# Hybrid decoder layer: second-layer input parts split from SBUF in two lumps, filler and early rows spread anew

## The chip, the core and the metric

The kernel runs on one core of a Trainium2 chip. The metric is the device time of one execution in microseconds (us); lower is better. One execution is also recorded by the hardware profiler, and its times are counted from the start of its span. The engines are named as in the profile: PE (TensorE, matmul), PEld (its weight loads), DVE (VectorE), ACT (ScalarE), POOL (GpSimd), SP (SyncE, which issues all the transfers of this kernel).

## The reference

One decoder layer over 1024 tokens of width 1024, all in float32:

```
h  = rmsnorm(x, g_pre);  proj = h @ W_in       # q,k,v of attention; q,f,i,g of the recurrence
A  = rmsnorm(dilated_attention(q_a, k_a, v_a)) # 8 heads of 64
     # three patterns (window, dilation): (128,1), (512,4), (2048,16), causal, ALiBi bias,
     # combined by their softmax denominators
R  = hgrn2(q_h, f_h, i_h, lb)                  # 4 heads of 128
     # S_t = diag(f_t) S_{t-1} + (1-f_t) i_t^T ; o_t = S_t^T q_t ; rmsnorm per head, times silu(g)
x  = x + rmsnorm(concat[A, R] @ W_out, g_post)
x  = x + rmsnorm(relu(rmsnorm(x, g_mlp) @ W1)^2 @ W2)     # W1: 1024 x 4096
```

## The kernel before

**Numbers and tiles.** A tile has 128 partitions. Each large product is made of three matmuls on two float32r parts of each operand, a rounded copy `hi` and the remainder `lo` (`three_pass`, L86 to L89: hi·hi, hi·lo, lo·hi). The parts are made by `split_into` (L82 to L84): a copy on ACT, then a subtraction on DVE. Weights come by SP into `raw`, are split into `wh` and `wl`, and the next one is loaded when a split has been issued (`w_split`, `w_get`); a weight either takes a rotating pair of `wh`/`wl`, or slabs named for it (`WO_TAG` for the eight blocks of W_out). Slabs are tiles of one size that several uses share one after the other: S 9, T 9, P 3, BT 2, V8 2, R 1, and eight larger ones ("A"). PSUM has four tags of two banks each: mm, s, t, pv.

**Order of the work.** The program is written out in order and each engine runs its part of it in that order. Work that isn't urgent, mostly projections, is a Python generator in `queue`. `fill(ns)` takes steps from it until their nominal costs (650 for three 128x512 matmuls) reach the amount; `drain()` takes all that is left. So `fill` and `drain` settle where the matmuls of the projections stand between those of the main work. A generator may also give up the turn when it has to wait for a place.

**Stages.** (1) Norm of the input and projections of head 0. (2) The four recurrence heads: `hgrn_core` (L373) makes the diagonal product `pd` from `prod` by eight small matmuls, then the levels within chunks (`pl`), transposes (`pk`), the states (`pu`, `st`), the outputs (`po`) in two groups and the gated norm; the filler is the next head's projections, and for the last head those of the first attention pair. Results go to `mix_dram` in DRAM. (3) Attention, 64 iterations, `s` = head times 8 + query block `b`, two heads to a pair. An iteration issues the exponential of block s+1 (`raise_`, ACT L577), the scores of s+2 (`look`, matmuls `ps` L563, maximum `mx` on DVE L566), the transposes of block s's probabilities (`turn`, `pt` L590, split into `pth` L593 on ACT and `ptl` L594 on DVE), every other iteration the weighted sum of values (`weigh`, `pov` L607, copied as `ot` L610), later the sum over two halves (`finish`, `fold` L618, L621), then a hook of that iteration and `fill`. The filler is `attn_proj`: V, K and Q of the next pair; K's half `kf` (L521) is split by ACT (`kh` L523) and POOL (`kl`), and copied to the other 64 partitions by four transfers. At the last iteration but one of a pair, `drain` runs ahead of the first scores of the next pair, which read `pairs`. (4) Output projection. The recurrence part of token blocks 0 to 3 is made early: `early_open` (L638) loads `erows` (L643), POOL multiplies them by the gain `gmix` (`row_rec` L658), PE transposes them (`row_turn`, `pmt` L698), and `early_out` makes the products `pwe` as filler in the last pair. Behind attention a loop over the eight token blocks makes the rest (`late_out`, `pwo`), the norm and residual (`residual`, `residual_b`, `esum` L775) and `next_turn`: transposes `ph` (L785) of the next layer's input, copied as `hraw` (L791), and for blocks 0 to 3 split into `h2` parts. (5), (6) The two feed-forward products, from L800 on; not touched.

The hooks at iterations 45 to 63 load the weights of W_out (`w_get(WO0 + k)`) and do the steps of (4) one by one.

Of the kernel before, what the change touches and what calls it, by code (L numbers as in the profile page):

```python
# [8 lines left out]
F32 = mybir.dt.float32  # L9
# [8 lines left out]
P = 128  # L18
# [7 lines left out]
AH = 8  # L26
# [4 lines left out]
def f32(ap):  # L31
    return ap.bitcast(F32)
# [3 lines left out]
def hymba_layer(ctx, tc, x, w_in, w_out, w_ff1, w_ff2, g_pre, lb_logits, g_mix, g_post,  # L36
# [40 lines left out]
    def rsqrt_mean(dst, ssum, n, width):  # L77
        t = col("ms", width)
        G.tensor_scalar(t, ssum, 1.0 / n, EPS, op0=ALU.mult, op1=ALU.add)  # L79
        G.tensor_tensor(out=dst, in0=t, in1=nhalf[:, :width], op=ALU.pow)  # L80
# [70 lines left out]
    for i in range(4 * HH, 4 * HH + 3 * (AH // 2)):  # L151
        stream.append((w_in[i], None))
    WO0 = len(stream)
    WO_TAG = (None, None, ("S", "S"), ("S", "BT"), ("S", "S"), ("S", "T"), ("T", "T"), ("T", "T"))

    def wo_dest(k, tags):
        return lambda: (slab(tags[0], f"woh{k}", F32R), slab(tags[1], f"wol{k}", F32R))
# [215 lines left out]
    def hgrn_core(h, scale, after=None):  # L373
        hd = heads[h]
        inat, gate, prod, qt, kt, tot = (hd[n] for n in ("inat", "gate", "prod", "qt", "kt", "tot"))
        fill(4500 * scale)
        pd = bank("t", f"pd{h}")
        for c in range(NT):
            TE.matmul(pd[:, c:c + 1], prod[:, c * P:(c + 1) * P], ones, start=True, stop=True)
# [3 lines left out]
        V.tensor_tensor(out=at, in0=ident.unsqueeze(1).to_broadcast([P, NT, P]),  # L383
                        in1=dg.unsqueeze(2).to_broadcast([P, NT, P]), op=ALU.mult)
        cur = tot
        for li, c in enumerate(LEVELS):
            nb = 64 // c
            qv = qt.rearrange("p (b two c) -> p b two c", two=2, c=c)
            kv = kt.rearrange("p (b two c) -> p b two c", two=2, c=c)
            av = at.rearrange("p n (b two c) -> p n b two c", two=2, c=c)  # L390
            pl = bank("s", f"pl{h}_{li}")
            for n in range(NT):
                TE.matmul(pl[:, n * 64:(n + 1) * 64], kt[:, n * P:(n + 1) * P],  # L393
                          qv[:, n * nb:(n + 1) * nb, 1, :], start=True, stop=True)
            w = T // (2 * c)
            cv = cur[:, :2 * w].rearrange("p (b two) -> p b two", two=2)
            V.tensor_tensor(out=kv[:, :, 0, :], in0=kv[:, :, 0, :],
                            in1=cv[:, :, 1:2].to_broadcast([P, w, c]), op=ALU.mult)
            V.tensor_tensor(out=qv[:, :, 1, :], in0=qv[:, :, 1, :],  # L399
                            in1=cv[:, :, 0:1].to_broadcast([P, w, c]), op=ALU.mult)  # L400
            nx = slab("P", f"tot{h}_{w}") if w > 64 else \
                tp.tile([P, w], F32, tag=f"tot{w}", name=f"tot{h}_{w}", bufs=1)
            V.tensor_tensor(out=nx[:, :w], in0=cv[:, :, 0], in1=cv[:, :, 1], op=ALU.mult)
            V.copy_predicated(
                av[:, :, :, 1, :],
                masks[:, li].rearrange("p (b c) -> p b c", c=c).unsqueeze(1).to_broadcast([P, NT, nb, c]),
                pl.rearrange("p (n b c) -> p n b c", n=NT, c=c))
            cur = nx
            fill(2900 * scale)
# [26 lines left out]
        for g4 in range(2):  # L436
            po = bank("pv", f"po{h}_{g4}").rearrange("p (n c) -> p n c", n=4)
            for j in range(4):
                n = g4 * 4 + j
                TE.matmul(po[:, j], at[:, n], inat[:, n], start=True, stop=n == 0)  # L440
                if n > 0:
                    TE.matmul(po[:, j], qt[:, n * P:(n + 1) * P], st[:, n], start=False, stop=True)
            g = slice(g4 * 4, g4 * 4 + 4)
            S.activation(sq[:, g], po, AF.Square)
            V.tensor_reduce(ss[:, g], sq[:, g], axis=AX.X, op=ALU.add)  # L445
            pos.append(po)
        rsqrt_mean(rs, ss, P, NT)
        if after is not None:
            after()
        fill(3000 * scale)  # L450
        for n in range(NT):
            V.scalar_tensor_tensor(gate[:, n], pos[n // 4][:, n % 4], rs[:, n:n + 1], gate[:, n],
                                   op0=ALU.mult, op1=ALU.mult)
# [8 lines left out]
    def attn_proj(pr):  # L462
# [48 lines left out]
        for hf in range(2):  # L511
            sl = slice(hf * 512, hf * 512 + 512)
            n = 0
            for cost in proj_t(w, f"ak{pr}", hf, box):
                n += 1
                if n == 3 and hf == 0:
                    v_turn(*late)
                    cost += 450.0
                yield cost
            full = half(f"kf{pr}{hf}")  # L520
            V.tensor_tensor(out=full, in0=box[0], in1=rrow[:, sl], op=ALU.mult)  # L521
            for i, (a, b) in enumerate(halves):
# [3 lines left out]
            for n in ("kh", "kl"):  # L526
                nc.sync.dma_start(out=f32(stacks[0][n][64:128, sl]), in_=f32(stacks[0][n][0:64, sl]))
                nc.sync.dma_start(out=f32(stacks[1][n][0:64, sl]), in_=f32(stacks[1][n][64:128, sl]))
            yield 650.0
        pairs[pr] = (stacks, vs)  # L530

    anats = [None] * (AH // 2)
    bts = {}
# [2 lines left out]

    def load_bias(hd):
        if hd < AH and hd not in bts:
            if hd < AH - 1:
                bts[hd] = slab("BT", f"bt{hd}")  # L540
            else:
                bts[hd] = wide.tile([P, 2, T], F32, tag="A", name=f"bt{hd}")[:, 0]
            nc.sync.dma_start(out=bts[hd], in_=bias_tab[hd])

    def score(hd, b):
# [89 lines left out]
    NE = 4  # L635
    early = {}

    def early_open():  # L638
        early["rows"] = wide.tile([P, NE, AW], F32, tag="A", name="erows")
        early["mt"] = [wide.tile([P, 2, 2, 4, P], F32R, tag="A", name=f"emt{q}") for q in range(NE // 2)]  # L640
        load_bias(AH - 1)
        early["sum"] = [wide.tile([P, 2, D], F32, tag="A", name=f"esum{q}") for q in range(NE // 2)]
        nc.sync.dma_start(out=early["rows"],  # L643
                          in_=mix_dram[:NE * P, :AW].rearrange("(n p) d -> p n d", p=P))

    def early_sum(t):
        return early["sum"][t // 2][:, t % 2]
# [7 lines left out]
        return early["rows"][:, t] if t < NE else rows[t][:, :AW]  # L655

    def row_rec(t):
        G.tensor_tensor(out=rec_row(t), in0=rec_row(t), in1=gains["gmix"][:, :AW], op=ALU.mult)  # L658

    def row_fin(t):  # L660
        return anats[-1][:, t].rearrange("p i d -> p (i d)")
# [115 lines left out]
    def next_turn(t):  # L777
# [3 lines left out]
        for kh in range(2):  # L781
# [7 lines left out]
                if th == 0:  # L789
                    h2[kh] = tuple(wide.tile([P, 4, 512], F32R, tag="A", name=f"h2{q}{kh}") for q in "hl")  # L790
            S.activation(hraw[kh, th][:, :, c:c + P], src, AF.Copy)  # L791
            if th == 0:
                hi, lo = (q[:, :, c:c + P] for q in h2[kh])
                split_into(hi, lo, src)

    steps = [(hd, b) for hd in range(AH) for b in range(NT)]
    scored, exped = {}, {}
# [19 lines left out]
    for h in range(HH):  # L817
# [6 lines left out]
            drain()  # L824

    hooks = {
        45: lambda: [drain(), load_gain("gmix", "R", g_mix), early_open()],
        46: lambda: w_get(WO0, 0),
        47: lambda: [w_get(WO0 + 1, 0), row_rec(0), row_rec(1)],
        48: lambda: [row_turn(0, 0), w_get(WO0 + 2, 0), row_rec(2), row_rec(3)],  # L830
        49: lambda: [row_turn(1, 0), w_get(WO0 + 3, 0), queue.extend(early_out(t) for t in range(NE))],
        50: lambda: row_turn(2, 0),
        51: lambda: row_turn(3, 0),
        55: lambda: [row_load(t) for t in range(3)],
        59: lambda: [row_norm(0), row_gain(0)],
        60: lambda: [row_norm(1), row_gain(1)],
# [6 lines left out]
    for s in range(n_steps):  # L843
# [10 lines left out]
            to_weigh.append((hd, b // 2))  # L854
        to_fold, last_fold = [(i, g, weigh(i, g)) for i, g in ready], to_fold
        if fresh and s + 2 < n_steps:
            drain()
            if (s + 2) // 16 + 1 < AH // 2:
                queue.append(attn_proj((s + 2) // 16 + 1))
            look(s + 2)  # L860
        for i, g, a in last_fold:
            finish(i, g, *a)
        hooks.get(s, lambda: None)()
        fill(2700.0 - 320.0 * b if s < n_steps - 16 else 1300.0)
    for i, g, a in to_fold:
        finish(i, g, *a)
    to_fold = [(i, g, weigh(i, g)) for i, g in to_weigh]
# [11 lines left out]
    for t in range(NT):  # L879
# [16 lines left out]
        if t + 3 < NT:  # L896
            row_norm(t + 3)
            if t + 3 < NE:
                row_gain(t + 3)
        if t == 4:  # L900
            w_get(W10, 0)
        mixed_half(t, 1)
# [758 lines left out]
```

## Time and profile before

| | |
|---|---|
| three runs | 1313.2, 1319.82, 1316.15 us |
| median | 1316.15 us |
| the profiled execution | 1313.2 us, span 1311.4 us (1.8 us lie around it) |
| PE busy | 1264.5 us, 96% of the span, 6730 matmul instructions |
| DVE, ACT, POOL busy | 858.7, 515.1, 283.6 us |
| mean granted clock over the span | 0.99 |

By the spans of the stages in the profiled execution, the recurrence heads run from about 42 to 300 us, the last of them ends near 336 us, attention runs until about 590 us, and the output projection until about 675 us.

In a row of instructions the first number is the time it starts (us), the second its duration; then engine, line, operation, `out<-in` with the program's names, shape, and in square brackets the time its engine had been idle just before and what it waited for last. A row of a group has its count, the busy time, the mean duration of one in ns, and the idle time before. The granted clock is the share of full speed at which TensorE was clocked in that stretch.

### The profile page before, as it was taken

To read this page: it belongs to the slowest core of one execution; us is meant where nothing else is said; L and a number is where in the kernel's file an instruction comes from. 1 tells how busy PE (TensorE), PEld (TensorE's weight loads), DVE (VectorE), ACT (ScalarE), POOL (GpSimd) and SP (SyncE) were. 2 spreads that over 40 slices of the span, in tenths; PEclk is the share of its full clock that TensorE was granted. 3 is DMA by queue.
4 is the path that set the end of the run, shared out by engine and by line. 5 is a ranking of instruction groups with operands and counts; after the bars stand their busy time and mean duration, and the time that the engine had idled before them with its cause. 6 is when DMAs were issued, how large, how long until landed. Compare 5 with 4: busy or idle time off the path is not lost. (4 is left out here: it accounts for less than half of the span.)

```text
span 1311.4 us, 17500 instructions
## 1 busy us (share of the span) xinstructions
PE 1264.5 (96%) x6730; PEld 1081.8 (82%) x6730; DVE 858.7 (65%) x1431; ACT 515.1 (39%) x908; POOL 283.6 (22%) x276
## 2 busy tenths in 40 slices
PE   9999999999989999898999899999999999999997
PEld 8898989888878888786887688888887888888886
DVE  5556566675656655666757656666666777688956
ACT  6612121213545554564555422222234633344412
POOL 0000000012011111123432178755651000000002
PEclk9999999999999999899999899999999999999999
DMA  5202020213122222416251444534469453444423
GB/s 203 65 17 65 17 64 17 65 49 98 48 81 65 81 65 59 137 41 215 97 177 58 143 168 169 177 129 140 174 222 347 165 196 115 146 131 128 147 80 130
DMA packets 58563, 153.77 MB, mean 117 GB/s; under 512 B 5104, under 2 KB 13040, under 8 KB 58224
## 3 DMA queue, kind: packets, MB, share of 16 engines
q1 hardware_dynamic: 58480, 152.66, 34.9%
q8 instruction: 53, 0.87, 0.3%
q14 instruction: 30, 0.25, 0.1%
HBM read 106.50 MB, written 39.85 MB: 112 GB/s over the span
## 5 line engine op out<-in xcount | busy, mean ns | idle before, releaser
L88 PE MATMUL f<-bl,ah 128*128 128x512 f32 x392 | 152.6, 389 | 0.5 <-DVE bl L84 0.5
L87 PE MATMUL f<-bh,ah 128*128 128x512 f32 x392 | 152.6, 389 | 0.4 <-ACT acc L1441 0.4
L89 PE MATMUL f<-bh,al 128*128 128x512 f32 x392 | 152.5, 389 | 0.0
L84 DVE TENSOR_TENSOR al<-ar,ah 128x1024 fp32r<-128x1024 f32 x49 | 60.7, 1239 | 49.6 <-ACT ah L83 21.7
L88 PEld LDWEIGHTS f<-bl,ah 128*128 128x128 f32 x392 | 73.6, 188 | 16.1 <-DVE bl L84 0.8
L87 PEld LDWEIGHTS f<-bh,ah 128*128 128x128 f32 x392 | 73.6, 188 | 16.0 <-ACT acc L1441 0.9
L89 PEld LDWEIGHTS f<-bh,al 128*128 128x128 f32 x392 | 73.6, 188 | 15.3
L83 ACT ACTIVATE ah<-ar 128x1024 fp32r<-128x1024 f32 x49 | 52.3, 1067 | 54.1 <-PE f L89 25.3
L566 DVE CUSTOM_DVE_ANT_0 p<-ps,bt 128x512 f32<-128x512 f32 (+2 forms) x96 | 50.6, 552 | 31.7 <-PE ps L564 31.5
L1577 POOL TENSOR_SCALAR fp<-fss 128x1 f32<-128x1 f32 x8 | 3.5, 432 | 268.8 <-ACT fd L1574 268.8
L594 DVE TENSOR_TENSOR ptl<-pt,pth 128x512 fp32r<-128x512 f32 (+2 forms) x96 | 50.2, 551 | 16.4 <-ACT pth L593 16.3
L593 ACT ACTIVATE pth<-pt 128x512 fp32r<-128x512 f32 (+2 forms) x96 | 43.3, 486 | 42.0 <-PE pt L590 41.8
L590 PE MATMUL pt<-ident,p 128*128 128x128 f32 x288 | 43.6, 279 | 11.6 <-DVE ptl L594 11.6
L393 PEld LDWEIGHTS pl<-qt,kt 128*128 128x128 f32 x448 | 52.9, 192 | 1.5 <-PE pm_av L89 0.9
L393 PE MATMUL pl<-qt,kt 128*128 128x64 f32 x448 | 53.5, 272 | 0.5 <-DVE qt L399 0.5
L577 ACT ACTIVATE p<-p,nm 128x128 f32<-128x128 f32 (+3 forms) x64 | 49.5, 773 | 10.0 <-DVE nm L572 5.7
L524 POOL TENSOR_TENSOR kl<-kf,kh 64x512 fp32r<-64x512 f32 x16 | 20.4, 1274 | 151.3 <-ACT kh L523 150.7
L231 ACT ACTIVATE inat<-pig,rstd 128x128 f32<-128x128 f32 x32 | 11.6, 367 | 95.4 <-PE pig L89 82.3
L590 PEld LDWEIGHTS pt<-ident,p 128*128 128x128 f32 x288 | 33.7, 142 | 17.2 <-DVE ptl L594 14.2
L83 ACT ACTIVATE bh<-br 128x1024 fp32r<-128x1024 f32 x28 | 29.9, 1067 | 41.1 <-PE f L89 35.8
L79 POOL TENSOR_SCALAR ms<-hss 128x8 f32<-128x8 f32 x4 | 0.8, 196 | 203.6 <-DVE hss L445 203.6
L84 DVE TENSOR_TENSOR wl<-raw,wh 128x1024 fp32r<-128x1024 f32 x23 | 31.3, 1359 | 18.0 <-ACT wh L83 18.0
(1584 smaller groups left out, 3848.9 us busy)
## 6 DMA issues: line engine op xcount, KB each, us to landing
ar<-actd SPq DMA_DIRECT2D x49, 512.0 KB, 3.7
raw<-in_w_in_dram SPq DMA_DIRECT2D x28, 512.0 KB, 3.7
w1r<-in_w_ff_dram SPq DMA_DIRECT2D x14, 1024.0 KB, 6.5
br<-in_w_ff_dram SPq DMA_DIRECT2D x14, 1024.0 KB, 6.5
actd<-e SPq DMA_DIRECT2D x17, 768.0 KB, 4.2
actd<-e SPq DMA_DIRECT2D x11, 1024.0 KB, 4.1
xr<-in_x_dram SPq DMA_DIRECT2D x8, 512.0 KB, 9.0
bt<-in_bias_tab_dram SPq DMA_DIRECT2D x8, 512.0 KB, 4.3
```

What stands on the lines that cost most here:

```text
L83: S.activation(hi, src, AF.Copy)
L84: eng.tensor_tensor(out=lo, in0=src, in1=f32(hi), op=ALU.subtract)
L87: TE.matmul(dst, lhs[0], rhs[0], start=start, stop=False)
L88: TE.matmul(dst, lhs[0], rhs[1], start=False, stop=False)
L89: TE.matmul(dst, lhs[1], rhs[0], start=False, stop=stop)
L393: TE.matmul(pl[:, n * 64:(n + 1) * 64], kt[:, n * P:(n + 1) * P], qv[:, n * nb:(n + 1) * nb, 1, :], start=True, stop=True)
L524: G.tensor_tensor(out=stacks[i]["kl"][a:b, sl], in0=full[a:b], in1=f32(stacks[i]["kh"][a:b, sl]), op=ALU.subtract)
L566: V.tensor_tensor_reduce(out=pe[:, k0:k0 + n], in0=pS[:, :n], in1=bts[hd][:, o:o + n], scale=1.0, scalar=-3.0e38, op0=ALU.add, op1=ALU.max ...
L577: S.activation(pe[:, :nk], pe[:, :nk], AF.Exp, bias=nm[:, b:b + 1], accum_out=dn[:, b:b + 1])
L590: TE.transpose(pt[:, j * P:(j + 1) * P], pe[:, jj * P:(jj + 1) * P], ident)
L593: S.activation(hi, src, AF.Copy)
L594: V.tensor_tensor(out=lo, in0=src, in1=f32(hi), op=ALU.subtract)
```

## The change

Six edits.

1. In `hgrn_core`, the filler ahead of `pd` is cut in two, one part now behind `pd`; that ahead of the gated norm is cut in two as well, one part now between the two groups of `po`.
2. Two blocks of W_out exchange where their parts lie.
3. In attention, an iteration's filler is 3400 - 360b in place of 2700 - 320b up to iteration 43, 1000 in 44 to 47, and 1300 from there on as before.
4. `pairs[pr]` is set just before the last step of the generator, and the pair's end calls the filler until it is set; it is drained only when another pair's projection follows.
5. The rows of blocks 0 to 3 are loaded by `early_rows`, called from within the last pair's projection after the first half of K, in two transfers, with a copy of the gain's first half of their own in a tile that head 7's bias shares; the hooks that follow move one or two iterations.
6. `next_turn` keeps only `hraw`; `split_tokens` splits two blocks at a time from SBUF in iterations 4 and 6 of the output loop.

```diff
-    WO_TAG = (None, None, ("S", "S"), ("S", "BT"), ("S", "S"), ("S", "T"), ("T", "T"), ("T", "T"))
+    WO_TAG = (None, ("S", "S"), None, ("S", "BT"), ("S", "S"), ("S", "T"), ("T", "T"), ("T", "T"))
...
-        fill(4500 * scale)
+        fill(2200 * scale)
         pd = bank("t", f"pd{h}")
...
         cur = tot
+        fill(2300 * scale)
         for li, c in enumerate(LEVELS):
...
             pos.append(po)
+            if g4 == 0:
+                fill(1500 * scale)
...
-        fill(3000 * scale)
+        fill(1500 * scale)
...
+            if hf == 0 and pr == AH // 2 - 1:
+                early_rows()
             full = half(f"kf{pr}{hf}")
...
+            pairs[pr] = (stacks, vs)
             yield 650.0
-        pairs[pr] = (stacks, vs)
...
-    def early_open():
+    def early_rows():
         early["rows"] = wide.tile([P, NE, AW], F32, tag="A", name="erows")
+        early["table"] = wide.tile([P, 2, T], F32, tag="A", name="etable")
         early["mt"] = [wide.tile([P, 2, 2, 4, P], F32R, tag="A", name=f"emt{q}") for q in range(NE // 2)]
-        load_bias(AH - 1)
+        gains["early"] = early["table"][:, 1, :AW]
+        nc.sync.dma_start(out=gains["early"], in_=g_mix[:AW].partition_broadcast(P))
+        for q in range(NE // 2):
+            nc.sync.dma_start(out=early["rows"][:, 2 * q:2 * q + 2],
+                              in_=mix_dram[2 * q * P:2 * (q + 1) * P, :AW].rearrange("(n p) d -> p n d", p=P))
+
+    def early_sums():
         early["sum"] = [wide.tile([P, 2, D], F32, tag="A", name=f"esum{q}") for q in range(NE // 2)]
-        nc.sync.dma_start(out=early["rows"],
-                          in_=mix_dram[:NE * P, :AW].rearrange("(n p) d -> p n d", p=P))
...
             S.activation(hraw[kh, th][:, :, c:c + P], src, AF.Copy)
-            if th == 0:
-                hi, lo = (q[:, :, c:c + P] for q in h2[kh])
-                split_into(hi, lo, src)
+
+    def split_tokens(kh, c):
+        hi, lo = (q[:, :, c:c + 2 * P] for q in h2[kh])
+        split_into(hi, lo, hraw[kh, 0][:, :, c:c + 2 * P])
...
-        45: lambda: [drain(), load_gain("gmix", "R", g_mix), early_open()],
-        46: lambda: w_get(WO0, 0),
-        47: lambda: [w_get(WO0 + 1, 0), row_rec(0), row_rec(1)],
-        48: lambda: [row_turn(0, 0), w_get(WO0 + 2, 0), row_rec(2), row_rec(3)],
-        49: lambda: [row_turn(1, 0), w_get(WO0 + 3, 0), queue.extend(early_out(t) for t in range(NE))],
-        50: lambda: row_turn(2, 0),
-        51: lambda: row_turn(3, 0),
+        45: lambda: [row_rec(0), row_rec(1)],
+        46: lambda: [w_get(WO0, 0), row_rec(2), row_rec(3)],
+        47: lambda: [row_turn(0, 0), w_get(WO0 + 1, 0), load_bias(AH - 1)],
+        48: lambda: [drain(), load_gain("gmix", "R", g_mix), early_sums(), w_get(WO0 + 2, 0), row_turn(1, 0),
+                     queue.extend(early_out(t) for t in range(NE))],
+        49: lambda: [w_get(WO0 + 3, 0), row_turn(2, 0)],
+        50: lambda: row_turn(3, 0),
...
         if fresh and s + 2 < n_steps:
-            drain()
+            while pairs[(s + 2) // 16] is None:
+                fill(1.0)
             if (s + 2) // 16 + 1 < AH // 2:
+                drain()
                 queue.append(attn_proj((s + 2) // 16 + 1))
             look(s + 2)
...
-        fill(2700.0 - 320.0 * b if s < n_steps - 16 else 1300.0)
+        fill(3400.0 - 360.0 * b if s < n_steps - 20 else 1000.0 if s < n_steps - 16 else 1300.0)
...
+        if t in (4, 6):
+            for kh in range(2):
+                split_tokens(kh, (t - 4) * P)
```

More of the change, by code (lines that the diff above doesn't have):

```diff
@@ L657, in row_rec @@
     def row_rec(t):
-        G.tensor_tensor(out=rec_row(t), in0=rec_row(t), in1=gains["gmix"][:, :AW], op=ALU.mult)
+        gain = gains["early"] if t < NE else gains["gmix"][:, :AW]
+        G.tensor_tensor(out=rec_row(t), in0=rec_row(t), in1=gain, op=ALU.mult)
     def row_fin(t):
```

5 lines of the change are left out of this document (1 added, 4 removed).

## The prediction

> **What bounds the kernel now.** I read the page's head first, then the stretches by engine and granted clock, then the chain of waits of TensorE. Columns of a stretch: its length; PE, PEld, DVE, ACT and POOL busy us with instructions; granted clock; DMA share; GB/s. A row of waits has the total, the count and the longest.
>
> ```profile
> span 1311.4 us, 17500 instructions
> ...
> PE 1264.5 (96%) x6730; PEld 1081.8 (82%) x6730; DVE 858.7 (65%) x1431; ACT 515.1 (39%) x908; POOL 283.6 (22%) x276
> ...
> L84 DVE TENSOR_TENSOR al<-ar,ah 128x1024 fp32r<-128x1024 f32 x49 | 60.7, 1239 | 49.6 <-ACT ah L83 21.7
> ...
> L83 ACT ACTIVATE ah<-ar 128x1024 fp32r<-128x1024 f32 x49 | 52.3, 1067 | 54.1 <-PE f L89 25.3
> ```
>
> ```profile
> 340.00:540.00 200.00, 183.56 (x1080) 160.22 (x1080) 116.22 (x371) 100.47 (x223) 30.55 (x24) 0.96 0.26 74
> 600.00:675.00 75.00, 70.01 (x345) 57.06 (x343) 50.75 (x69) 38.51 (x104) 27.14 (x58) 1.00 0.37 126
> ```
>
> ```profile
> PE pt L590 <- DVE ptl L594: 11.6, 7, 2.8
> ```
>
> TensorE is busy 96% of the span, and the change removes no matmul. Time can come only from TensorE's gaps and from its clock. The attention stretch holds 16.4 idle us at a mean clock of 0.96, and the gaps there have names: seven waits of the probability transposes `pt` for `ptl`, the low half of the block before, and the wait of `pmt` for POOL (part 5). All of them sit where a pair of heads ends and the generator queue has run dry or is drained at once. I go through the places in order of time; a plus is time gained.
>
> **1. Recurrence.** The 4500 of filler before the diagonal product `pd` become 2200 before and 2300 behind it.
>
> ```profile
> 130.26 0.28 PE L87 MATMUL pig<-wig2h,hTh 128*128 128x256 f32 x1
> ...
> 132.78 0.28 PE L87 MATMUL pig<-wig2h,hTh 128*128 128x256 f32 x1
> 132.95 0.69 DVE L369 TENSOR_TENSOR prod<-qt,kt 128x512 f32<-128x512 f32 x1
> ```
>
> The `pig` matmuls of the filler run from 130.26 to 132.78, 21 in all. The second half of `prod`, which `pd` needs, ends at 132.95 + 0.69 = 133.64. With half of the filler gone, `pd` is reached some 0.36 early: an estimate, the rest of the first half and four `pd` before it being taken off the 3.4 us between. Three heads have filler: 3 x 0.36 = -1.1. The low bound is -3 x 0.69, a whole `prod` each; the high bound is 0, since TensorE had work here and nothing it waited for. The second split, 3000 into 1500 and 1500 around the group of `po`, keeps the same matmuls under the same norms: 0. If that cover were gone, it would cost the 0.69 of one such vector operation.
>
> **2. Opening of attention.** The first iterations get 3400 in place of 2700, which is two groups of three 128x512 matmuls more, by 650 each.
>
> ```profile
> 128.45 0.39 PE L88 MATMUL pm_f<-hTl,wh 128*128 128x512 f32 x1
> 128.68 0.39 PE L89 MATMUL pm_f<-hTh,wl 128*128 128x512 f32 x1
> ...
> 336.27 0.50 PE L563 MATMUL ps<-kh,q 128*128 128x512 f32 x1 [2.28 <-DVE mx L566]
> ```
>
> A 128x512 matmul starts every 0.23 us. Six more of them fill 6 x 0.23 = 1.4 of the 2.28 in front of `ps`: +1.4. Bounds 0 (another wait behind it) and 2.28.
>
> **3. First pair change.** K of the next pair is now complete two iterations before the score that needs it; the loop calls the filler only until `pairs` is set and drains the rest later, so that V and Q of the pair after stay as filler.
>
> ```profile
> 370.29 1.28 ACT L523 ACTIVATE kh<-kf 64x512 fp32r<-64x512 f32 x2 [1.72 <-DVE kf L521]
> 371.60 1.04 ACT L577 ACTIVATE p<-p,nm 128x896 f32<-128x896 f32 x1
> ...
> 373.25 1.02 DVE L594 TENSOR_TENSOR ptl<-pt,pth 128x512 fp32r<-128x512 f32 x2 [1.53 <-ACT pth L593]
> 374.00 0.98 PE L590 MATMUL pt<-ident,p 128*128 128x128 f32 x7 [1.75 <-DVE ptl L594]
> ```
>
> ```profile
> 384.35 2.00 DVE L84 TENSOR_TENSOR wl<-raw,wh 128x1024 fp32r<-128x1024 f32 x1 [2.04 <-ACT wh L83]
> 387.54 0.33 PE L590 MATMUL pt<-ident,p 128*128 128x128 f32 x1 [2.85 <-DVE ptl L594]
> ```
>
> The copies `kh` stand on ScalarE ahead of the exponential, so `ptl` comes late and `pt` waits 1.75. That chain is unchanged. A group of three matmuls that stood in the gap is gone: 3 x 0.23 = 0.7, and the gap grows to about 2.4. Four iterations on, `wl` no longer runs in front of `ptl` with POOL beside it (2.00 us here, against the mean of 1.24 in the group row above), and the filler is not dry: the 2.85 goes. Sum -0.7 + 2.85 = +2.2; bounds -2.85 (both waits stay and a third comes) and +4.6.
>
> **4. Second pair change, and the blocks between.**
>
> ```profile
> 411.98 0.44 PE L590 MATMUL pt<-ident,p 128*128 128x128 f32 x2 [1.02 <-DVE ptl L594]
> ...
> 455.49 0.48 PE L590 MATMUL pt<-ident,p 128*128 128x128 f32 x1 [2.85 <-DVE ptl L594]
> ...
> 522.12 1.26 PE L590 MATMUL pt<-ident,p 128*128 128x128 f32 x7 [1.94 <-DVE ptl L594]
> ```
>
> The 1.02 stands here and once more in the next pair (the seven waits: 1.75 + 2.85 + 1.02 + 2.85 + 1.02 + 1.94 + a small one = 11.6). Both have 360 more filler in the iteration, and their weight split moves ahead: +2.0, bounds 0 and 2.0. The change itself gives back 2.85 at 455.49 and gets a gap like the first's, 2.4, where K now ends: +0.4, bounds -2.4 and +2.85. Together +2.4.
>
> **5. Third pair change and the early rows.** A gap of 2.4 is new at the end of K; 1.94 at 522.12 goes.
>
> ```profile
> 523.32 0.38 SPq L643 DMA_DIRECT2D erows<-mixd  x1
> ...
> 530.96 3.73 POOL L658 TENSOR_TENSOR erows<-erows,gmix 128x512 f32<-128x512 f32 x3 [9.33 <-DMA erows<-mixd]
> 532.28 1.11 PE L698 MATMUL pmt<-ident,erows 128*128 128x128 f32 x4 [4.70 <-POOL erows L658]
> ```
>
> ```profile
> raw<-in_w_out_dram SPq DMA_DIRECT2D x3, 512.0 KB, 4.4
> erows<-mixd SPq DMA_DIRECT2D x1, 1024.0 KB, 7.5
> ```
>
> The rows are now loaded when half of K of the last pair is made, in two transfers, with their own slice of the gain (a broadcast of 128x512). Both are issued several iterations ahead of use, more than the 7.5 us that the one transfer takes, so POOL's product is ready and the 4.70 goes. Without filler in that iteration the first two `pmt` will still wait for the pair's end; I take 1.5 (1.02 and half of it), bounds 0 and 2 x 1.94. The three new issues on SP cost 0.38 each and stand ahead of the stack transfers of K, needed a whole iteration later: 0. The fourth block of W_out is asked for later than before and takes 4.4; its two splits (means 1.07 and 1.24) follow, and the first `pwe` needs it. Of these 6.7 us, scores, transposes and the weighted sum of the iteration cover some 4.6; I take -2.1, bounds 0 and -4.4. Sum: -2.4 + 1.94 + 4.7 - 1.5 - 2.1 = +0.6.
>
> **6. End of attention.** `early_out` ends one iteration sooner. Its last six matmuls, which stood between the last copy `ot` and the fold, are gone: the fold follows at once.
>
> ```profile
> 587.93 0.39 ACT L610 ACTIVATE ot<-pov 128x256 f32<-128x256 f32 x1 [1.60 <-PE pov L607]
> 589.11 0.55 PE L618 MATMUL pov<-fold,ot 128*128 128x64 f32 x4
> ```
>
> From `ot` to the fold lie 1.2 us, now bare: -1.2; bounds -1.6 (what the copy itself waited for `pov`, once more), and 0 if the copy is early enough.
>
> **7. Slabs.** Block 1 of W_out takes the two S slabs and block 2 the rotating pair, the other way round than before; head 7's bias shares a tile with the early gain and is loaded at iteration 47, nine ahead of its first score; the tiles of the sums open later. Nine iterations are some 38 us (340 to 600 holds about 62), which hide the load: 0. Without them it would cost a transfer like the 4.4 above.
>
> **8. h2 from SBUF.** The hi/lo split per token of the second layer's input leaves iterations 2 to 5 of the output loop and comes as two lumps at token 4 and 6, each 128x4x256 for two halves.
>
> ```profile
> 616.10 0.69 DVE L84 TENSOR_TENSOR h2l<-ph,h2h 128x512 fp32r<-128x512 f32 x1 [1.84 <-ACT h2h L83]
> ...
> 619.11 1.06 PE L785 MATMUL ph<-ident,esum 128*128 128x128 f32 x8 [2.25 <-DVE esum L775]
> 620.98 0.50 PE L87 MATMUL pwo<-wh,mt 128*128 128x512 f32 x1 [0.80 <-ACT mt L83]
> ...
> 647.36 0.47 PE L87 MATMUL pwo<-wh,mt 128*128 128x512 f32 x1 [0.43 <-DVE ad L762]
> ```
>
> VectorE waited 1.84 for ScalarE's `h2h`, then spent two times 0.69 before it could make `esum`: 3.2 us, more than the 2.25 that `ph` waits. So the 2.25 goes, most of the 0.80 (0.5) and the 0.43: +3.2. The lumps are 2 x 1.07 on ScalarE and 2 x 1.24 on VectorE, in a stretch where these are busy 38.5 and 50.8 of 75 us. They fit; if the 2.5 of VectorE stood wholly ahead of a residual, the next `pwo` would wait 1.4 (2.5 less one six-matmul group). Bounds +1.8 and +3.5.
>
> Sum of waits: -1.1 + 1.4 + 2.2 + 2.4 + 0.6 - 1.2 + 3.2 = **+7.5**.
>
> **9. Clock.**
>
> ```profile
> 451.06:454.47 3.41, 1.58 (x14) 1.26 (x11) 2.17 (x2) 2.53 (x6) 2.08 (x2) 1.00 0.53 125
> 454.47:457.88 3.41, 2.39 (x11) 2.40 (x12) 2.86 (x13) 0.88 (x3) 0.00 (x0) 0.50 0.96 292
> 457.88:461.30 3.42, 3.42 (x13) 2.95 (x12) 0.00 (x0) 0.98 (x3) 0.00 (x0) 0.50 0.12 47
> ...
> 382.80:386.20 3.40, 1.89 (x16) 1.57 (x15) 1.85 (x1) 2.85 (x6) 2.40 (x2) 1.00 0.51 118
> 386.20:389.60 3.40, 2.06 (x18) 2.06 (x19) 3.18 (x14) 0.88 (x3) 0.00 (x0) 1.00 0.91 272
> ...
> 522.70:526.10 3.40, 3.40 (x17) 3.21 (x17) 2.82 (x12) 3.06 (x8) 0.00 (x0) 0.51 0.92 234
> ...
> 532.90:536.40 3.50, 3.50 (x16) 3.20 (x15) 2.09 (x2) 2.50 (x6) 3.02 (x3) 0.50 0.00 0
> ```
>
> The gap at 455.49 lies mostly in one stretch of 3.41 us (1.83 idle), and the next two run at 0.50. The equal gap at 387.54 falls across a border (1.51 and 1.34 idle), and the clock stays at 1.00. Half of the busy time is lost at 0.50: (2.39 + 3.42 + 3.40 + 3.50) / 2 = 6.4 at three places. After: three gaps of 2.4, each inside one stretch with a chance of about 2.4 / 3.41 = 0.7, at 2.1 a time: 4.4. Gain +2.0. The Trainium skill's page "TensorE: Matmul & The Clock Gate" (HAM oscillation) asks for no idle gap above some 3.4 us. By that rule no gap here would cost clock, before or after, and this term would be 0 in place of +2.0; the trace disagrees, since 2.85 and 1.94 us were enough.
>
> Together 9.5: 1313.2 - 9.5 = 1303.7 for a run like the profiled one. That run was the fastest of three, 3 below their median; with fewer gaps near the clock's border I let that distance nearly halve (+1.8): median **1305.5**.
>
> **Rivals.** *About the same, 1312.* The three ends without filler also stall at the last block of each pair, as at 522.12: 3 x 1.94 = 5.8, and every new gap costs clock (4.4 becomes 6.3): 1305.5 + 5.8 + 1.9 = 1313, or 1312 when one finds cover. For it: two iterations per change have no filler at all. Against it: there the copies of K are already done. *Faster still, 1301.* No gap reaches the clock's border: 1305.5 - 4.4. For it 387.54, against it 455.49. The Trainium skill's rule of part 9 would give the same after the change. *Slower, 1323.* Iterations without filler run at the speed of the chain exponential, `pth`, `ptl`, and two more waits of 2.4 come at each change: 6 x 2.4 = 14.4, and the gain in clock is gone with 3 more losses at 1 each: 1305.5 + 17.4 = 1323. It decides from about seven extra waits, (1322.7 - 1305.5) / 2.4. For it: 1.75 stood there with filler; against it: before, too, some iterations had little.
>
> **How the numbers follow.** The forecast (1302 to 1309) has 0.52, the same 0.22, faster still 0.12, slower 0.14. Half a per cent is 6.6 us, about what a measurement can tell, so faster means under 1309.6 and slower over 1322.7. Of the forecast 0.04 lies above 1309.6. Faster 0.60, same 0.26, slower 0.14. The range 1298 to 1318 leaves out most of the slower case and a little of the fastest, some 0.17.
>
> **What would show it.** Right: no `pmt` wait for POOL over 2 us; no `pt` wait of 2.85; three of about 2.4, one at each end of K; `ph` without 2.25; granted clock from 340 to 540 above 0.96. Wrong: rows `pt` with more than five waits, a `pwe` that waits over 4 us for `woh3`, a `pwo` that waits for the lumps, or a `pd` that waits over 0.7.

## The result, and the profile after

The median of 13 runs is 1308.23 us (1304.69 to 1312.50), against 1315.22 us of the kernel before in as many runs beside it. The ratio is 0.9943, with a 95% interval of 0.9927 to 0.9959: 0.57% faster, where 0.8% was forecast. The profiled execution is one of 1308.23 us. The profile before is of an execution of 1313.2 us, 2.0 under the median of its runs, so the two profiles differ by less (5.0 us of span) than the medians (7.0).

The head of the page of the changed kernel, and its attention stretch (columns as in the prediction):

```profile
span 1306.4 us, 17483 instructions
...
PE 1262.8 (97%) x6730; PEld 1081.0 (83%) x6730; DVE 859.5 (66%) x1427; ACT 516.9 (40%) x904; POOL 281.1 (22%) x276
```

```profile
340.00:540.00 200.00, 186.85 (x1116) 163.11 (x1115) 125.23 (x397) 107.03 (x232) 30.65 (x25) 0.98 0.30 85
```

TensorE's waits in the changed kernel: total, count, longest.

```profile
PE pt L592 <- DVE ptl L596: 7.5, 3, 2.5
...
PE ps L565 <- DVE mx L568: 2.7, 3, 0.9
...
PE pd L379 <- DVE prod L369: 2.0, 2, 1.0
...
PE pmt L708 <- issue: 1.3, 2, 0.8
...
PE pwe L87 <- ACT woh L83: 0.9, 1, 0.9
...
PE pwe L88 <- DVE wol L84: 0.8, 1, 0.8
```

The seven waits of `pt` (11.6 in all) are three of 2.5, one per pair. The 4.7 of `pmt` for POOL and the 2.25 of `ph` are gone. New are two waits of `pd`, two of `pwe`, and two of 0.9 of `ps`, one in each of the next two pairs at the place where the first has it at the opening (341.86, 409.42 and 476.95 us, 67.5 apart).

To see where the time went, both traces are cut at four instructions of TensorE: the first `pm_q` behind head 0's projections, the group of `pl` in the last head that waits for `qt` (the expectations call it the last head's first `pl`; those that count from the first wait of `po` begin 28.1 us later), the first `pwo` behind attention, the first `f11a` of the feed-forward. Before, and then after:

```profile
42.42 0.50 PE L87 MATMUL pm_q<-hTh,wh 128*128 128x512 f32 x1 [0.48 <-DVE gate L232]
...
284.56 1.97 PE L393 MATMUL pl<-qt,kt 128*128 128x64 f32 x16 [0.52 <-DVE qt L399]
...
589.86 0.47 PE L87 MATMUL pwo<-woh,mt 128*128 128x512 f32 x1
...
674.66 0.39 PE L1029 MATMUL f11a<-h2h,wh 128*128 128x512 f32 x1
```

```profile
44.03 0.50 PE L87 MATMUL pm_q<-hTh,wh 128*128 128x512 f32 x1 [0.48 <-DVE gate L232]
...
290.17 1.97 PE L394 MATMUL pl<-qt,kt 128*128 128x64 f32 x16 [0.52 <-DVE qt L400]
...
587.27 0.47 PE L87 MATMUL pwo<-woh,mt 128*128 128x512 f32 x1
...
669.64 0.39 PE L1046 MATMUL f11a<-h2h,wh 128*128 128x512 f32 x1
```

| stretch | before | after | difference | predicted |
|---|---|---|---|---|
| to `pm_q` | 42.42 | 44.03 | +1.6 | 0 |
| recurrence, `pm_q` to `pl` | 242.14 | 246.14 | +4.0 | +1.1 |
| last head and attention, `pl` to `pwo` | 305.30 | 297.10 | -8.2 | -7.4 |
| output projection, `pwo` to `f11a` | 84.80 | 82.37 | -2.4 | -3.2 |
| the rest | 636.74 | 636.76 | 0.0 | 0 |
| span | 1311.4 | 1306.4 | -5.0 | -9.5 |

The first stretch isn't touched by the change. In the other profiled kernels, which share it, it took 41.4 to 42.9 us, so the 1.6 is this execution's; a wait of 0.75 of `xt` for a transfer of the input, which the profile before doesn't have, is part of it. The real miss is the recurrence: 2.0 us of idle time in front of `pd`, and a stretch at half clock behind the second wait. How much of the latter belongs to the change, one execution doesn't say; the run with the attention filler alone comes back to it.

### The profile page after: what moved, and what is told of

It is laid out like the page before. It is cut to its first block, busy times and chain, and to the rows that moved or that the text cites. A ratio compares the mean times of both kernels' runs of the same rounds, so it can differ in the third digit from the quotient of the medians.

```text
span 1306.4 us, 17483 instructions
## 1 busy us (share of the span) xinstructions
PE 1262.8 (97%) x6730; PEld 1081.0 (83%) x6730; DVE 859.5 (66%) x1427; ACT 516.9 (40%) x904; POOL 281.1 (22%) x276
## 5 line engine op out<-in xcount | busy, mean ns | idle before, releaser
L595 ACT ACTIVATE pth<-pt 128x512 fp32r<-128x512 f32 (+2 forms) x96 | 43.4, 486 | 43.2 <-PE pt L592 42.9
L568 DVE CUSTOM_DVE_ANT_0 p<-ps,bt 128x512 f32<-128x512 f32 (+2 forms) x84 | 44.3, 552 | 23.4 <-PE ps L566 23.0
L398 DVE TENSOR_TENSOR kt<-kt,tot 128x512 f32<-128x512 f32 x28 | 20.2, 721 | 35.7 <-PE pl L394 35.7
```

The source lines that it names most:

```text
L568: V.tensor_tensor_reduce(out=pe[:, k0:k0 + n], in0=pS[:, :n], in1=bts[hd][:, o:o + n], scale=1.0, scalar=-3.0e38, op0=ALU.add, op1=ALU.max ...
L595: S.activation(hi, src, AF.Copy)
```

## The experiments

The ratios are to runs of the kernel before on the same chip; all cuts are those of the table, taken from one profiled execution each.

**Filler ahead of pd whole again, in the changed kernel.**

```diff
-        fill(2200 * scale)
+        fill(4500 * scale)
...
-        fill(2300 * scale)
```

> The changed kernel with the filler ahead of pd whole again (4500, none behind pd). Theory: the two waits of pd for prod (0.95 and 1.01 us) and the stretch at about half clock after the second one (1.7 us lost) are the split's own price, so pm_q of head 0 to the first pl of the last head takes 242.1 us as in the kernel before, in place of 246.1, and the kernel is 2 to 4 us faster than the changed one (about 1305). Rival: the half behind pd covered waits of the levels; then new waits of pl or pk of 1 us or so per head appear and the time stays at 1308.

```profile
42.52 0.50 PE L87 MATMUL pm_q<-hTh,wh 128*128 128x512 f32 x1 [0.48 <-DVE gate L232]
...
284.81 1.97 PE L393 MATMUL pl<-qt,kt 128*128 128x64 f32 x16 [0.53 <-DVE qt L399]
```

Measured 1302.26 us, ratio 0.9910 (0.9892 to 0.9928). The recurrence takes 242.29 us, 3.85 less than in the changed kernel. No wait of the levels appears, so the half behind `pd` covered nothing that shows. Of the 3.85, 2.0 are the two waits of `pd`; the rest is the half-clock stretch, which isn't in this profile.

**The split around pd alone, in the kernel before.**

```diff
-        fill(4500 * scale)
+        fill(2200 * scale)
...
         cur = tot
+        fill(2300 * scale)
```

> The kernel before with only the split 2200 / 2300 around pd. Theory: pd waits about 1.0 us for prod in each of two heads, so the recurrence takes 2.0 us more, and 1.7 more for each of the two after which the clock falls: 1317 to 1320. Rival: pd is reached only 0.36 us early, as predicted, and the wait seen in the changed kernel comes from another of its edits: 1316.

```profile
42.48 0.50 PE L87 MATMUL pm_q<-hTh,wh 128*128 128x512 f32 x1 [0.48 <-DVE gate L232]
...
285.07 1.97 PE L394 MATMUL pl<-qt,kt 128*128 128x64 f32 x16 [0.51 <-DVE qt L400]
```

Measured 1314.33, ratio 0.9996 (0.9973 to 1.0019). The recurrence takes 242.59 us, and `pd` has no wait of 0.4 or more. The theory fell, the rival was nearer: between these two executions the split by itself costs less than half a microsecond, so the waits in the changed kernel needed a second cause.

**The other split undone, in the changed kernel.** The only other edit in the recurrence is 3000 into 1500 and 1500.

```diff
-            if g4 == 0:
-                fill(1500 * scale)
...
-        fill(1500 * scale)
+        fill(3000 * scale)
         for n in range(NT):
```

> The changed kernel with the filler of 3000 ahead of the gated norm whole again; the split around pd stays. Theory after the runs so far: neither split alone makes pd wait; with only 1500 ahead of it, the gated norm stands on VectorE waiting for POOL's hrs while prod of the next head queues behind it, and the half behind pd is missed only then. So pm_q of head 0 to the first pl of the last head takes 242.6 us, as with the pd split alone, no pd waits over 0.4, and the time is that of e1 (1302). Rival: the pd split costs its 2 us in the changed kernel whatever stands ahead of the norm: 246 and 1307.

The second head's norm, `prod` and `pd` in the changed kernel, and then here. POOL's `hrs` is what the norm (`gate`) waits for.

```profile
127.36 2.16 DVE L455 SCALAR_TENSOR_TENSOR gate<-po,hrs,gate 128x128 f32<-128x128 f32 x8 [2.04 <-POOL hrs L80]
...
135.62 0.69 DVE L369 TENSOR_TENSOR prod<-qt,kt 128x512 f32<-128x512 f32 x1
...
136.37 1.05 PE L379 MATMUL pd<-ones,prod 128*128 128x1 f32 x8 [0.95 <-DVE prod L369]
```

```profile
124.96 2.16 DVE L453 SCALAR_TENSOR_TENSOR gate<-po,hrs,gate 128x128 f32<-128x128 f32 x8
...
133.04 1.98 PE L379 MATMUL pd<-ones,prod 128*128 128x1 f32 x16
...
133.22 0.69 DVE L369 TENSOR_TENSOR prod<-qt,kt 128x512 f32<-128x512 f32 x1
```

Measured 1300.06, ratio 0.9872 (0.9858 to 0.9887); recurrence 242.57 us, no wait of `pd`. With 1500 moved between the two groups of `po`, the second group, and with it POOL's `hrs`, comes later and less filler follows: VectorE stands 2.04 us waiting for POOL, and `fr`, `kt` and `prod` of the next head queue behind it; with 3000 it doesn't wait. Counted from `pm_q`, the second half of `prod` starts at 91.59 us in the changed kernel and at 90.63 here, 0.96 earlier, while `pd` is reached at 90.44 and 90.45: the delay is as long as the wait. With the longer filler ahead of `pd`, the late `prod` is covered: in the first experiment VectorE waits the same 2.04, and `pd` doesn't. The two splits cost together what neither costs alone.

The split of the 3000 has a second price. In the last head its first 1500 stands ahead of `open_attention`, which drains the queue anyway, so the next pair's projection gets that much less ahead of attention. All profiles with both the new attention filler and the split have the 0.9 of `ps` at the opening; without the split (here and in the attention filler alone) the opening has no wait, and the first pair's end has 1.15 and 1.06 in place of 2.5. That adds to the gain.

**h2 from SBUF alone, in the kernel before** (edit 6 of the change, nothing else).

```diff
-            if th == 0:
-                hi, lo = (q[:, :, c:c + P] for q in h2[kh])
-                split_into(hi, lo, src)
...
+        if t in (4, 6):
+            for kh in range(2):
+                split_tokens(kh, (t - 4) * P)
```

> The kernel before with only the split of h2 from SBUF in iterations 4 and 6. Theory: the waits of ph (2.25) and of the next pwo (0.80, 0.43) go, and the lumps are hidden: from the last fold of attention to the first f11a 3 us less than before, 1312. Rival: the lumps delay a pwo by 1.4 us, and the gain is 1.8 or less. Second rival: the gain of this stretch in the changed kernel (3.4 us) came from the earlier end of early_out, and here it is 0.

```profile
590.55 0.47 PE L87 MATMUL pwo<-woh,mt 128*128 128x512 f32 x1
...
672.03 0.39 PE L1033 MATMUL f11a<-h2h,wh 128*128 128x512 f32 x1
```

The output projection takes 81.48 us, 3.3 less than before, and no `ph` waits for `esum`. Whole runs give 1311.85, ratio 0.9982 (0.9955 to 1.0008), which can't tell 3 us from none; the cut can: the ten profiles with this edit that were cut have 81.2 to 82.4 us here, and the four without it 84.8 to 86.6. The lumps are hidden. In the changed kernel the gain is 2.4: a `pwo` waits 0.9 for `mt` there, 0.4 here.

**The attention filler alone, in the kernel before.** This ran after the next experiment, which its expectation names.

```diff
-        fill(2700.0 - 320.0 * b if s < n_steps - 16 else 1300.0)
+        fill(3400.0 - 360.0 * b if s < n_steps - 20 else 1000.0 if s < n_steps - 16 else 1300.0)
```

> The kernel before with the changed amounts of filler in attention and nothing else of the change. Theory: these amounts carry nearly all of the gain in attention (waits of 2.85 at two pair ends, 1.02 twice and 1.94 go, three of 2.5 come), and the wait of pmt for POOL falls from 4.7 to about 2.6 by itself; from the first po wait to the first pwo some 268 us, as in e6, in place of 277.2, and about 1307. Rival: the earlier completion of a pair (edit 4) is what takes the waits away; then this stretch stays within 2 us of 277.

```profile
PE pt L590 <- DVE ptl L594: 7.6, 5, 2.5
PE pmt L698 <- POOL erows L658: 3.4, 1, 3.4
```

Measured 1304.35, ratio 0.9926 (0.9902 to 0.9950): with this one line alone the kernel can't be told from the whole change. `pl` to `pwo` takes 583.57 - 288.45 = 295.1 us, 10.2 less than before. The wait for POOL falls from 4.7 to 3.4 by itself, with the rows asked for in iteration 45 as before; why wasn't tried. The earlier setting of `pairs` and the smaller drain aren't needed for the gain.

The recurrence is, line for line, that of the kernel before, and takes 246.71 us in this execution for 242.14, with no wait of `pd`: three stretches of half clock, one behind `pd` and `pl` of the second head, two behind those of the third:

```profile
201.13 1.84 PE L379 MATMUL pd<-ones,prod 128*128 128x1 f32 x16
202.83 3.01 PE L393 MATMUL pl<-qt,kt 128*128 128x64 f32 x16
```

```profile
203.50:210.20 6.70, 6.70 (x33) 6.70 (x33) 4.51 (x7) 0.74 (x2) 0.00 (x0) 0.50 0.08 34
```

So a half-clock stretch in the recurrence of one execution proves nothing about the splits. The 2.0 of idle time does: both profiles with the two splits and no longer filler ahead of `pd` have it (the changed kernel, and the next experiment), and none of the others.

**Early rows as before, in the changed kernel** (edits 2 and 5 undone: `early_open` with one transfer and the gain `gmix`, and the old hooks).

```diff
-        45: lambda: [row_rec(0), row_rec(1)],
-        46: lambda: [w_get(WO0, 0), row_rec(2), row_rec(3)],
...
+        45: lambda: [drain(), load_gain("gmix", "R", g_mix), early_open()],
+        46: lambda: w_get(WO0, 0),
+        47: lambda: [w_get(WO0 + 1, 0), row_rec(0), row_rec(1)],
...
```

> The changed kernel with the early rows loaded as in the kernel before (hook 45, one transfer, the gain gmix, the old hooks and slabs); the fillers of attention stay as changed. Theory: pmt waits 4 to 5 us for POOL's erows again, with a half-clock stretch behind it, and the two waits of pwe for the fourth block of W_out (1.7 together) go: 3 to 5 us more than the changed kernel from the first po wait to the first pwo (272 to 274 in place of 269.0), about 1312. Rival: the wait only moves, to the end of K or to pwe, and the stretch stays at 269 to 270.

```profile
PE pmt L701 <- POOL erows L661: 2.6, 1, 2.6
PE pd L379 <- DVE prod L369: 2.0, 2, 1.0
```

Measured 1310.18, ratio 0.9943 (0.9924 to 0.9962), the same as the whole change. `pl` to `pwo` takes 584.89 - 289.10 = 295.8 us, 1.3 less than with the early rows. The theory fell: what is left to gain is 2.6 us plus some tenths at `pmt`, and the changed kernel pays 1.3 at `pmt` and 1.7 at `pwe` for it. The 1.3 can be the clock's: between these cuts the changed kernel has two stretches of half clock, this profile one.

**kh one iteration after kf** (with the filler ahead of `pd` whole, as in the first experiment). This asks what the three remaining waits of 2.5 are.

```diff
             V.tensor_tensor(out=full, in0=box[0], in1=rrow[:, sl], op=ALU.mult)
+            if pr > 0 and hf == 1:
+                yield None
             for i, (a, b) in enumerate(halves):
                 S.activation(stacks[i]["kh"][a:b, sl], full[a:b], AF.Copy)
```

> As e1_no_pd_split, and for pairs 1 to 3 the copies kh of the second half of K are written one iteration later than kf. Theory: the wait of 2.5 us of pt at the end of K comes from kh, which waits for kf on ScalarE ahead of the exponential; without that wait the three gaps of pt are under 1.0 each, 4.5 us or more are gained, and half-clock stretches there go too: about 1299. Rival: these iterations have too little work for TensorE and wait for ptl whatever stands on ScalarE; then the gap stays over 2 or moves to the next pt, and the time equals that of e1.

The end of K in the changed kernel (`nm` is the maximum that the exponential at 380.94 needs), and then the same wait and the stretch here:

```profile
376.90 0.21 DVE L574 TENSOR_SCALAR nm<-mx 128x1 f32<-128x1 f32 x1
...
379.63 1.28 ACT L528 ACTIVATE kh<-kf 64x512 fp32r<-64x512 f32 x2 [1.72 <-DVE kf L526]
...
380.94 1.04 ACT L579 ACTIVATE p<-p,nm 128x896 f32<-128x896 f32 x1
...
383.33 0.98 PE L592 MATMUL pt<-ident,p 128*128 128x128 f32 x7 [2.50 <-DVE ptl L596]
```

```profile
378.17 0.98 PE L593 MATMUL pt<-ident,p 128*128 128x128 f32 x7 [0.88 <-DVE ptl L597]
```

```profile
340.00:540.00 200.00, 192.24 (x1171) 167.73 (x1170) 129.27 (x417) 112.24 (x243) 30.78 (x24) 1.00 0.29 85
```

Measured 1297.37, ratio 0.9867 (0.9853 to 0.9882). All three waits fall from 2.5 to 0.9, and the clock is 1.00 in attention. The chain named in the prediction is shown: `kh` waits for `kf` on ScalarE, ahead of an exponential whose maximum was there at 377.11. Against the first experiment, `pl` to `pwo` falls from 296.9 to 289.8: 4.9 by the three waits, the rest by the clock, for that profile has two stretches of half clock in attention.

**Two steps further.** On the kernel of the undone 3000 split with `kh` later, the four products of the early rows together in iteration 45:

```diff
-        45: lambda: [row_rec(0), row_rec(1)],
-        46: lambda: [w_get(WO0, 0), row_rec(2), row_rec(3)],
+        45: lambda: [row_rec(t) for t in range(4)],
+        46: lambda: w_get(WO0, 0),
```

> As e5, with kh one iteration later than kf for pairs 1 to 3 and the products of all four early rows in iteration 45, ahead of kl on POOL. Theory: as e4 (1297.4), less the 1.19 of pmt for erows; 1296. Rival: the four products (5 us on POOL) hold up kl, then the stacks' transfers, and the first scores of the last pair wait: over 1298.

Measured 1297.61, ratio 0.9853 (0.9836 to 0.9869), no better than the one before. The first `pmt` waits 1.19 still; POOL isn't what it waits for last any more, so that reading was wrong. Another stands in the rows:

```profile
515.11 0.69 DVE L596 TENSOR_TENSOR ptl<-pt,pth 128x512 fp32r<-128x512 f32 x1 [0.52 <-ACT pth L595]
...
515.90 0.63 PE L708 MATMUL pmt<-ident,erows 128*128 128x128 f32 x4 [1.19 <-issue]
```

`pmt` starts 0.10 us after the first half of `ptl` ends. It does so in the changed kernel (0.11), in the `kh` experiment (0.10) and in the next kernel (0.10) too, though the waits are 0.8 to 1.8. `pmt` takes its bank from the PSUM tag `t`, whose two banks the `pt` of the block before fill and `ptl` reads, so it has to wait until `ptl` has read one. No run gave `pmt` another bank; this is read from the rows and the program, not tested.

The splits of W_out blocks 0 to 3 one iteration sooner as well:

```diff
-        45: lambda: [row_rec(t) for t in range(4)],
-        46: lambda: w_get(WO0, 0),
-        47: lambda: [row_turn(0, 0), w_get(WO0 + 1, 0), load_bias(AH - 1)],
...
+        45: lambda: [row_rec(t) for t in range(4)] + [w_get(WO0, 0)],
+        46: lambda: w_get(WO0 + 1, 0),
+        47: lambda: [row_turn(0, 0), w_get(WO0 + 2, 0), load_bias(AH - 1)],
...
```

> As b1, with the splits of W_out blocks 0 to 3 one iteration sooner (45 to 48). Theory: the waits of pwe for woh and wol (0.61 and 0.77) go: 1295. Rival: the splits (1.07 on ScalarE and 1.24 on VectorE each) stand ahead of the exponential and of ptl in iterations without filler, and pt waits more than that: 1297 or more.

Measured 1294.84, ratio 0.9835 (0.9820 to 0.9850). The waits of `pwe` are gone, and the first `pmt` waits 1.8 in place of 1.2, since a split of W_out now runs on VectorE ahead of `ptl`: of 1.4 us 0.8 stays.

With the filler ahead of `pd` whole and that ahead of the norm split (the kernel of the `kh` experiment with these hooks):

> As e4 (filler ahead of pd whole, kh later) with the hooks of b2: all four products of rows in iteration 45, the splits of W_out blocks 0 to 3 in iterations 45 to 48. Theory: the waits of pwe (1.4 in e4) go as in b2, and the first pair's gap stays 0.9 in place of b2's 2.0: 1294 or a little under, the fastest of all. Rival: e4's advantage in the profile was the clock's luck at one gap, and it equals b2 or is slower.

Measured 1295.46, ratio 0.9837 (0.9801 to 0.9872): not told from the last. Its profile has 0.9 at the first pair's end in place of 2.0, and loses 1.7 in the last head, where TensorE has no gap at all:

```profile
268.84:272.25 3.41, 3.41 (x10) 2.69 (x10) 3.41 (x5) 0.00 (x0) 1.45 (x1) 0.52 0.36 82
```

The `kh` experiment had lost as much there; the next two ask why, and whether it can be mended.

**What lowers the clock: pd six times, in the kernel before.**

```diff
-        for c in range(NT):
+        for c in 6 * list(range(NT)):
             TE.matmul(pd[:, c:c + 1], prod[:, c * P:(c + 1) * P], ones, start=True, stop=True)
```

> The kernel before with the eight matmuls of one column of pd written six times in each of the four heads (the same sums again), so that TensorE runs nothing but these and the narrow pl for some 8 us without a gap. Theory: what lowers the clock is little work in a stretch of 3.41 us, and matmuls of one column count as hardly any, though the profile shows TensorE busy; then the granted clock is about 0.5 in one or two stretches behind each pd, and the recurrence takes 5.3 us for each head more and 1.7 or 3.4 on top. Rival: only idle time counts; then the granted clock is 1.00 from 42 to 300 us.

The matmuls of the first head, and the stretches around them (the third row is the part of the second in which only `pd` runs):

```profile
70.26 15.57 PE L379 MATMUL pd<-ones,prod 128*128 128x1 f32 x96
```

```profile
70.20:75.20 5.00, 5.00 (x47) 5.00 (x47) 0.21 (x1) 0.00 (x0) 0.00 (x0) 1.00 0.33 108
75.20:92.20 17.00, 17.00 (x83) 17.00 (x83) 4.21 (x6) 0.37 (x1) 0.00 (x0) 0.51 0.00 0
75.20:85.60 10.40, 10.40 (x53) 10.40 (x52) 0.00 (x0) 0.00 (x0) 0.00 (x0) 0.52 0.00 0
92.20:150.00 57.80, 57.80 (x406) 53.71 (x405) 33.77 (x67) 12.98 (x22) 1.83 (x2) 1.00 0.12 37
```

It ran once: 1384.39 us, a span of 1382.6. TensorE is busy 17.00 of 17.00 us, and is granted 0.51; for 10.4 of them it runs only matmuls of one column. Five us of these bring the clock down without any idle time; it comes back some 7 us after the last of them, when `pl` and a few wide matmuls have run. All four heads show it. The price was underrated: 17.8 us a head by the spans, where at most 8.7 were forecast, as the matmuls then run at half speed themselves.

**A short split around pd.** As the last kernel of the two steps (filler ahead of `pd` whole, `kh` later, W_out sooner), with wide matmuls between `pd` and `pl`:

```diff
-        fill(4500 * scale)
+        fill(3800 * scale)
...
         cur = tot
+        fill(700 * scale)
```

> As b3, with 3800 of filler ahead of pd and 700 behind it, so that wide matmuls stand between pd and the narrow pl. Theory: the stretch of low clock behind pd and pl of the last head (1.7 us lost in the profiled executions of e4 and b3) can't come any more, and pd finds prod ready: from pm_q to the last head's first pl 242.6 us, 1294. Rival: pd is reached before prod, as in the changed kernel, and waits 0.3 or more in each of two heads, and nothing is gained: 1295.5 or more.

```profile
42.37 0.50 PE L87 MATMUL pm_q<-hTh,wh 128*128 128x512 f32 x1 [0.48 <-DVE gate L232]
...
284.57 1.97 PE L394 MATMUL pl<-qt,kt 128*128 128x64 f32 x16 [0.52 <-DVE qt L400]
```

Measured 1293.37 (1291.30 to 1294.09), ratio 0.9833 (0.9811 to 0.9854): the fastest median, 1.7% under the kernel before, though not told from the two others of this group by the interval. The recurrence takes 242.20 us, with no wait of `pd` over 0.4 and no low clock. Other profiles have none there without this split (the first experiment), so one execution doesn't show that the wide matmuls are what keeps the clock up.

## Why the prediction was right, and where it was not

The forecast named the sign and most of the places; 1308.23 lies in its range and 2.7 above its number: 7.0 us of gain for 10.7.

- *Part 1, recurrence: wrong.* The step that failed is "the second split ... keeps the same matmuls under the same norms: 0". It moved 1500 of filler from the place where VectorE's norm waits for POOL, and delayed `prod` behind it. With the pd split the wait is 0.95 and 1.01 in two heads, not 0.36 in three: 2.0 for 1.1. In the recurrence each split alone is harmless, as two runs show. Most of the rest of the +4.0 is a stretch of half clock behind the second wait, which this execution had and another without any split had too. In the last head, where nothing was booked, the second split took filler from the opening of attention.
- *Part 2, opening: the number right by luck.* The row of 2.28 became 0.91, as 1.4 less gives. But with the attention filler alone the wait goes altogether; the 0.91 is what the second split of part 1 gives back.
- *Parts 3 and 4, pair ends: right in mechanism and size.* Three waits of 2.5 were forecast as 2.4, one at each end of K; 2.85 twice, 1.02 twice and 1.94 went. Not foreseen: 0.9 of `ps` in each of the next two pairs, 1.8 together. That these gains come from the amounts of filler, and not from `pairs` being set earlier, the prediction left undecided; the run with that line alone decides it.
- *Part 5, early rows: the sum right, the reason not.* Forecast at `pmt` 1.5, measured 1.3, and by the rows it is a bank of PSUM that it waits for; at `pwe` 2.1, measured 1.7. But the 4.7 that it booked as gained is partly the filler's: with old rows and new filler 2.6 to 3.4 is left of it. What the early rows earn by themselves is about nothing.
- *Part 6, end of attention.* The fold now waits 0.5 for `ot`; 1.2 was too much.
- *Part 8, h2: right.* +3.2 forecast, 3.3 alone and 2.4 in the whole change. The low bound has a slip: 2.5 less a six-matmul group of 1.4 is 1.1, not 1.4; the sum doesn't use it.
- *Part 9, clock: sum near by luck, rule incomplete.* Three losses were forecast as 2.1 of 3 gaps. The profile has one of the three gaps, one behind the waits of `pwe`, and one in the recurrence:

```profile
204.50:207.91 3.41, 3.41 (x20) 3.41 (x18) 1.23 (x2) 0.00 (x0) 0.00 (x0) 0.53 0.53 154
...
518.40:521.82 3.42, 3.42 (x17) 3.42 (x18) 1.94 (x7) 1.71 (x4) 3.42 (x4) 0.52 0.19 45
...
535.60:539.01 3.41, 3.41 (x17) 3.27 (x16) 1.75 (x7) 1.09 (x3) 0.00 (x0) 0.53 0.89 312
```

That is 3 x 3.41 x 0.47 = 4.8 for 4.4. The two gaps of 2.5 at the first and second pair cost no clock: a border of the 3.41 us stretches cuts them into 0.94 and 1.56, and 1.67 and 0.83, while 2.41 of the third gap lie in one. The chance of 0.7 was worked out the wrong way round: 2.4 / 3.41 is the chance that a border falls into the gap, and that it lies wholly inside one stretch has 0.3. By the count at the end of this document some 1.9 us in one stretch are enough, which gives an estimate of 0.6. Here one of the three gaps cost clock; the two other losses, at `pwe` and in the recurrence, weren't foreseen. The remark that by the cited rule no gap here would cost clock overlooks the 4.70 of `pmt` before, which is longer than the 3.4 us that it names.

Of the rivals, the slower one is out: only the three waits that were forecast stand at the pair ends. The one of "about the same" is out in its mechanism, as the last block of a pair doesn't stall; the faster one too, since the clock still fell.

## What to carry to other kernels

Moving filler is not free where it covers another engine's wait: ask for each block of it which vector or scalar operation waits beside it, and what queues behind that operation, and cost two such moves together. A wait at the end of a projection can be a copy that stands in order ahead of an urgent operation on another engine; letting it go one iteration later took 1.6 off each of three waits. Where whole runs spread by more than the effect, cutting the traces at the same instructions tells a microsecond, once the half-clock stretches in each cut have been looked at: with the same instructions and no wait of `pd`, one recurrence took 246.7 us and another 242.1.

## What the hardware did that was not expected

The granted clock fell to 0.52 with TensorE busy 10.40 of 10.40 us, when all that it ran were matmuls of one column (the run with `pd` six times). A shorter case is in the profile of the attention filler alone: no gap of 0.4 or more in the recurrence, and yet 246.7 us for 242.1, with 0.50 to 0.52 behind `pd` and `pl` of two heads. So the busy time of the profile isn't what the clock follows; narrow matmuls count for little. The Trainium skill's page "TensorE: Matmul & The Clock Gate" (Part 1: The HAM clock gate) speaks of an activity window of some 3.4 us that runs freely; stretches of that length at 0.50 to 0.53 agree with it. In each of the fourteen profiles the clock changes only at whole steps of 3.41 us from one another. Laid on these steps, a gap of TensorE between 40 and 700 us that lies 1.92 us or more in one step is always followed by half clock (19 cases); none that lies 1.50 to 1.75 us in one is (16 cases); of those with 1.79 to 1.90, five are and two are not. Whether the spread between runs of one kernel comes from where `pd` and the gaps fall in these windows wasn't tried.
